# Block products with sums on both sides in the down projections of a two-layer trunk

## The chip, the cores and the metric

The kernel runs on one core of a Trainium2 chip. The metric is the device time of one execution in microseconds, and the median of three runs stands for a kernel. The core has five engines that matter here, each with a queue of its own that it works through in order: TensorE (PE in the profile, its weight loads apart as PEld), VectorE (DVE), ScalarE (ACT), GpSimd (POOL) and SyncE (SP), which issues the loads.

## What is computed

A trunk of two layers over 256 rows (tokens) of 1024 numbers, all in float32. Each layer has a feed-forward block, a token mixer and a second feed-forward block, each between two RMS norms:

```python
def swiglu(h, w_gate_up, w_down):
    gu = h @ w_gate_up                      # 1024 x 5632
    g, u = jnp.split(gu, 2, axis=-1)
    return (jax.nn.silu(g) * u) @ w_down    # 2816 x 1024

for l in range(DEPTH):                      # DEPTH = 2
    h = swiglu(rms_norm(x, ffn1_pre[l]), ffn1_w_gate_up[l], ffn1_w_down[l])
    x = x + 0.5 * rms_norm(h, ffn1_post[l])
    h = hybrid_mixer(rms_norm(x, mix_pre[l]), ...)
    x = x + rms_norm(h, mix_post[l])
    h = swiglu(rms_norm(x, ffn2_pre[l]), ffn2_w_gate_up[l], ffn2_w_down[l])
    x = x + 0.5 * rms_norm(h, ffn2_post[l])
```

The change lies in the four products with `w_down` (the down projections) and in the norm after every block. The mixer (a gated convolution, causal pooling, their projections and an output projection) is as it was, but its output projection goes through the same function.

## The kernel before

**Precision.** Every float32 operand is split into two float32r parts, `hi` (a rounded copy, made by ScalarE) and `lo` (the rest, `raw - hi`, made by VectorE). A product is the sum of three matmuls: hi·hi, hi·lo and lo·hi. Weights are split as they arrive, activations (`split`, `split_pair`) as they are made.

**The weight stream.** All weights of the program form one list of chunks (`stream`, line 89), each 128 partitions x 2048 numbers (1 MB). `issue` (line 108) takes the next chunk of the list: it takes a buffer `hi` and a buffer `lo` (pools `whi` and `wlo`, `LOOK + 1` = 5 buffers each), has SP load the chunk as two halves into two `raw` buffers (pool `raws`, 5 buffers of 128x1024), and puts the splits, a copy on ScalarE and a subtraction on VectorE for each half, into the list `parts`. These are written into the queues of the two engines later, one at a time by `part` between other work, or all of them when `chunk` asks for the next weights. So where a split stands among VectorE's other work is fixed by this code, and a `raw` buffer can take its next load only after its split. `chunk` (line 135) hands out the weights of the next chunk and issues loads until the five buffers are spoken for (`top_up`).

**A feed-forward block** (`ffn`, line 351). Eleven chunks of 256 hidden numbers (`NFU`). For each, two `feat_product` calls (gate and up, 32 matmuls each), sums from PSUM (`add_up`), silu, a multiplication, and `split_pair`, which writes the activations for the down projection into a buffer of the pool `acts`. Then `out_product` (line 275) multiplies: a chunk has two halves of 128 rows of `w_down` (`kk`), two blocks of 128 tokens (`b`) and two halves of 512 output columns (`h`), and each of these eight `step`s is three matmuls of 512 columns, so 24 matmuls a chunk. The results stay in four PSUM banks, `banks[b][h]`, of eight. The first eight chunks go one after the other. The last three (`TAIL`) are held together, so that block 0 is finished first and its norm (`on_block`, which calls `post` and `pre`) runs while TensorE does block 1.

**The norm after a block** (`post`, line 209). ScalarE sums squares of the two banks, VectorE multiplies each bank with a gain into an SBUF tile `u`, POOL makes the reciprocal root `r`, and VectorE computes `x = u * r + x`.

The order on each engine is that of the code (`InOrder`, line 41). The scheduler beneath it only gives out buffers and sets the waits.

Of the kernel before, what the change touches and what calls it, by code (L numbers as in the profile page):

```python
# [10 lines left out]
F32 = mybir.dt.float32  # L11
F32R = mybir.dt.float32r
# [21 lines left out]
WARM = 16  # L34
TURN0 = (9, 11)


F_BG, F_CW, F_PB, F_PS, F_N = 0, 16, 40, 48, 56

# [13 lines left out]
def trunk(ctx: ExitStack, tc: tile.TileContext, x, gains, gcol, feat, wgu1, wd1, win, wco, wpg, wpo, wo, wgu2, wd2, out):  # L53
# [14 lines left out]
    def bank():  # L68
        return psum.tile([P, 512], F32, name="ps")
# [20 lines left out]
    for l in range(DEPTH):  # L90
        for wgu, wd in ((wgu1, wd1), (wgu2, wd2)):
            if wgu is wgu2:
                stream += [("in", l, c) for c in (16, 17, 18, 19)]
                for j in range(4):
                    stream += [("in", l, 4 + j), ("in", l, 8 + j), ("in", l, j)]
                stream += [("in", l, c) for c in (12, 13, 14, 15, 20, 21, 22, 23)]
                stream += [("pg", l, 0)]
                stream += [("co", l, j) for j in range(4)]
                stream += [("po", l, j) for j in range(4)]
                stream += [("o", l, j) for j in range(4)]  # L100
            n = 1 if wgu is wgu1 else 2
            stream += [(f"gu{n}", l, c) for c in range(2 * NFU)]
            stream += [(f"d{n}", l, c) for c in range(NFU)]
    src = {"gu1": wgu1, "d1": wd1, "gu2": wgu2, "d2": wd2, "in": win, "co": wco, "pg": wpg, "po": wpo, "o": wo}
    ready = {}
    state = {"issued": 0, "used": 0}

    def issue(now=True):

        i = state["issued"]  # L110
        state["issued"] = i + 1
        name, l, c = stream[i]
        hi = whi.tile([P, CHUNK], F32R, name="hi")
        lo = wlo.tile([P, CHUNK], F32R, name="lo")
        h = CHUNK // 2
        for s in range(2):
            sl = slice(s * h, (s + 1) * h)
            raw = raws.tile([P, h], F32, name="raw")
            nc.sync.dma_start(raw, src[name][l, c, :, sl])
            parts.append(lambda sl=sl, raw=raw: act.copy(hi[:, sl], raw))  # L120
            parts.append(
                lambda sl=sl, raw=raw: dve.tensor_tensor(lo[:, sl], raw, hi[:, sl].bitcast(F32), op=ALU.subtract)
            )
        ready[i] = (hi, lo)
        if now:
            part(4)

    parts = []

    def part(n=1):  # L130
        for _ in range(n):
            if parts:
                parts.pop(0)()

    def chunk(name, held=0):

        i = state["used"]
        assert stream[i][0] == name, (stream[i], name)
        state["used"] = i + 1
        top_up(held + 1)  # L140
        if state["issued"] == i + 1:
            part(len(parts))
        return ready.pop(i)

    def top_up(held):


        part(len(parts))
        while state["issued"] < min(state["used"] + LOOK + 1 - held, len(stream)):
            part(len(parts))  # L150
            issue(False)

# [115 lines left out]
    def split_pair(src_ap):  # L268
# [6 lines left out]
    def out_product(name, nchunk, acts_hl, on_block):  # L275
        banks = [[bank(), bank()] for _ in range(NB)]
        last = 2 * nchunk - 1

        def step(b, h, kt, w, kk):
            ts_ = slice(b * P, (b + 1) * P)  # L280
            wh, wl = (t.rearrange("p (k c) -> p k c", c=D)[:, kk, HALF[h]] for t in w)
            _, ah, al = acts_hl[kt]
            o = banks[b][h]
            pe.matmul(o, ah[:, ts_], wh, start=(kt == 0), stop=False)
            pe.matmul(o, ah[:, ts_], wl, start=False, stop=False)
            pe.matmul(o, al[:, ts_], wh, start=False, stop=(kt == last))

        for c in range(nchunk - TAIL):
            w = chunk(name)
            for kk in range(2):  # L290
                for b in range(NB):
                    for h in range(2):
                        step(b, h, 2 * c + kk, w, kk)
        ws = []
        for h in range(2):
            for c in range(TAIL):
                if len(ws) <= c:
                    ws.append(chunk(name, c))
                for kk in range(2):
                    step(0, h, 2 * (nchunk - TAIL + c) + kk, ws[c], kk)  # L300
        on_block(0, banks[0])
        n = 0
        for cs in (range(1), range(1, TAIL)):
            for h in range(2):
                for c in cs:
                    for kk in range(2):
                        step(1, h, 2 * (nchunk - TAIL + c) + kk, ws[c], kk)
# [43 lines left out]
    def ffn(l, gu, dn, acts_hl, on_block, gains_):  # L351
# [9 lines left out]
        hs = []  # L361
        for f in range(2, NFU):
            ps = feat_product(gu, acts_hl)
            if f == 2:
                hs += split_pair(turn_back(tok[0]))
            sil = add_up(ps, "sil")
            act.activation(sil, sil, AF.Silu)
            ps = feat_product(gu, acts_hl)
            if f == 2:
                hs += split_pair(turn_back(tok[1]))  # L370
            h = add_up(ps, "h")
            dve.tensor_tensor(h, h, sil, op=ALU.mult)
            hs += split_pair(h)
        gains_()
        out_product(dn, NFU, hs, on_block)

    def mixer(l, acts_hl, on_block, gains_):
        ft = small.tile([P, F_N], F32, name="ft", bufs=1)
# [97 lines left out]
            dve.tensor_tensor(z, z, ga[j], op=ALU.add)  # L476
            merged += split_pair(z)
        gains_()
        out_product("o", 4, merged, on_block)


    plan = []
# [81 lines left out]
    return np.ascontiguousarray(w).reshape(l, k // (2 * P), P, CHUNK)  # L564


def _fill(chunks, at):

    l = chunks.shape[0]
# [45 lines left out]
```

## Time and profile before

| | |
|---|---|
| median of three runs | 1179.0 us (1178.93 to 1180.57) |
| the profiled execution, its own time | 1179.98 us |
| its span, from the first to the last instruction | 1178.2 us |
| TensorE busy | 1165.9 us (99%) |
| VectorE busy | 803.8 us (68%) |
| ScalarE busy | 640.6 us (54%) |
| matmuls | 6192 |
| loaded and stored | 225.00 MB, 191 GB/s over the span |

"Busy" counts an instruction from its start to its end, and in a row of such instructions each begins some 0.08 us before the one ahead of it ends, so that the pace of a row is shorter than the time of one instruction. Line 49 is the wrapper `InOrder`, so instructions are told apart by their tiles: `ps` a PSUM bank, `hi`, `lo` and `raw` weights, `act` activations for an output product, `xt` those for a gate or up product.

### The profile page before, as it was taken

What the parts mean: (1) busy time and instruction counts of PE and PEld (TensorE: products, weight loads), DVE (VectorE), ACT (ScalarE), POOL (GpSimd) and SP (SyncE); (2) the same over time, 40 slices, a digit from 0 to 9 for tenths busy, and PEclk for the clock granted to TensorE, in tenths of its full rate; (3) what the DMA queues carried; (4) which work ended last, traced back from release to release, by engine and by line L of the source; (5) the groups of instructions that cost most, each with busy time, mean ns of one, the idle gap of its engine ahead of it and who ended that gap; (6) DMA issues with size and microseconds to landing.
All of it is one profiled execution on the core that took longest, in us unless ns stands there. A gap on an engine that the chain in (4) does not pass through costs nothing.

```text
span 1178.2 us, 16248 instructions
## 1 busy us (share of the span) xinstructions
PE 1165.9 (99%) x6192; PEld 1002.5 (85%) x6192; DVE 803.8 (68%) x1093; ACT 640.6 (54%) x990; POOL 17.2 (1%) x75
## 2 busy tenths in 40 slices
PE   8999999999999999999999999999999999999997
PEld 5888888888898888888888888888888988888886
DVE  5676745587988777675476766466789886676742
ACT  6655634665565565554365555356556565555630
POOL 0000000000000000000000000000000000000000
PEclk9999999999999999999999999999999999999999
DMA  8666663655566574656456566546565655666540
GB/s 299 216 198 193 194 224 130 245 167 180 170 202 208 169 263 162 193 184 234 159 188 205 182 197 229 189 141 208 178 203 187 200 181 176 200 198 197 190 164 36
DMA packets 62574, 225.00 MB, mean 191 GB/s; under 512 B 7328, under 2 KB 7328, under 8 KB 62496
## 3 DMA queue, kind: packets, MB, share of 16 engines
q1 hardware_dynamic: 62352, 223.96, 57.6%
q8 instruction: 49, 0.80, 0.3%
q14 instruction: 29, 0.24, 0.1%
q10 hardware_dynamic: 144, 0.00, 0.0%
HBM read 222.88 MB, written 1.05 MB: 190 GB/s over the span
## 4 chain that ended last, share of the span: by engine, by line
PE 97%; DVE 1%; ACT 1%; DMA 1%; issue 0%; POOL 0%; SPq 0%; DVEq 0%; POOLq 0%; ACTq 0%
PE ps L49 97%; DVE lo L49 1%; DMA raw<-in_wgu 1%; ACT hi L49 0%; ACT xt L49 0%; ACT junk L49 0%; POOL r L200 0%; DVE x L49 0%; DVE xn L49 0%; DVE v L49 0%; SPq L78 0%; DVEq L611 0%; DVE xt L49 0%; DVE u L49 0%; POOLq L611 0%
## 5 line engine op out<-in xcount | busy, mean ns | idle before, releaser
L49 DVE TENSOR_TENSOR lo<-raw,hi 128x1024 fp32r<-128x1024 f32 x412 | 494.4, 1220 | 134.6 <-ACT hi L49 134.1
L49 ACT CAST hi<-raw 128x1024 fp32r<-128x1024 f32 x412 | 424.5, 1050 | 114.6 <-PE ps L49 89.1
L49 PE MATMUL ps<-xt,hi 128*128 128x512 f32 x1792 | 428.3, 391 | 0.0
L49 PEld LDWEIGHTS ps<-xt,hi 128*128 128x128 f32 x1792 | 329.6, 188 | 64.2
L49 PE MATMUL ps<-hi,act 128*128 128x512 f32 x832 | 259.8, 390 | 0.0
L49 PEld LDWEIGHTS ps<-xt,lo 128*128 128x128 f32 x1792 | 229.8, 191 | 8.7
L49 PE MATMUL ps<-xt,lo 128*128 128x256 f32 x1792 | 232.5, 283 | 0.0
L49 PEld LDWEIGHTS ps<-hi,act 128*128 128x128 f32 x832 | 156.2, 188 | 32.0
L49 PE MATMUL ps<-lo,act 128*128 128x512 f32 x416 | 161.9, 389 | 0.0
L49 ACT COPY h<-ps 128x256 f32<-128x256 f32 x136 | 49.6, 372 | 129.1 <-PE ps L49 128.9
L49 DVE TENSOR_TENSOR h<-ps,h 128x256 f32<-128x256 f32 x136 | 56.2, 422 | 74.7 <-ACT h L49 74.6
L49 PE MATMUL ps<-hi,xt 128*128 128x512 f32 x384 | 100.5, 396 | 3.3 <-ACT hi L49 2.0
L49 PEld LDWEIGHTS ps<-lo,act 128*128 128x128 f32 x416 | 78.2, 188 | 15.7
L49 ACT COPY sil<-ps 128x256 f32<-128x256 f32 x120 | 43.6, 375 | 83.7 <-PE ps L49 83.7
L49 PEld LDWEIGHTS ps<-hi,xt 128*128 128x128 f32 x384 | 71.8, 190 | 18.5 <-ACT hi L49 2.3
L49 PE MATMUL ps<-act,hi 128*128 128x512 f32 (+1 forms) x320 | 72.6, 369 | 0.0
L49 DVE TENSOR_TENSOR sil<-ps,sil 128x256 f32<-128x256 f32 x104 | 42.3, 421 | 42.0 <-ACT sil L49 42.0
L49 ACT CAST act<-h 128x512 fp32r<-128x512 f32 x60 | 37.3, 621 | 60.4 <-DVE h L49 60.4
L49 PEld LDWEIGHTS ps<-act,hi 128*128 128x128 f32 x320 | 57.0, 189 | 9.1
L49 PE MATMUL ps<-lo,xt 128*128 128x512 f32 x192 | 53.9, 399 | 1.2 <-DVE lo L49 1.2
L49 DVE TENSOR_TENSOR act<-h,act 128x512 fp32r<-128x512 f32 (+1 forms) x68 | 46.6, 685 | 6.0 <-ACT act L49 5.7
L49 PEld LDWEIGHTS ps<-lo,xt 128*128 128x128 f32 x192 | 35.8, 189 | 11.3 <-DVE lo L49 4.2
(59 smaller groups left out, 467.4 us busy)
## 6 DMA issues: line engine op xcount, KB each, us to landing
raw<-in_wgu SPq DMA_DIRECT2D x176, 512.0 KB, 4.6
raw<-in_win SPq DMA_DIRECT2D x96, 512.0 KB, 4.7
raw<-in_wd SPq DMA_DIRECT2D x88, 512.0 KB, 4.6
raw<-in_wco SPq DMA_DIRECT2D x16, 512.0 KB, 4.9
raw<-in_wpo SPq DMA_DIRECT2D x16, 512.0 KB, 3.9
raw<-in_wo SPq DMA_DIRECT2D x16, 512.0 KB, 4.7
gain<-in_gains SPq DMA_DIRECT2D x11, 512.0 KB, 4.7
raw<-in_wpg SPq DMA_DIRECT2D x4, 512.0 KB, 3.9
```

Source lines behind the costliest of these rows:

```text
L49: return lambda *a, **kw: self.tc.keep_in_program_order(f(*a, **kw))
```

## The change

Four of the eleven chunks of every down projection (`FAST` = 2, 4, 6, 8) are multiplied in another way. The 256x256 activations and the 256x1024 weights of such a chunk are seen as 2x2 blocks. Seven block products with sums of blocks on both sides replace eight, in the scheme of Strassen and Winograd. So such a chunk has 21 matmuls in place of 24. For this

- VectorE makes four sums of 128x128 of the activations (`forms`), and seven activation blocks are split in place of four;
- VectorE makes four sums of 128x512 of the weights, in place in the two `raw` buffers, after three of the four blocks have been split, and then the buffers are split once more: seven blocks in place of four. Such a chunk takes two buffers of `whi` and `wlo` (`cost` is 2);
- the products go to eight banks in place of four (`extra` holds four of them). The chunks are taken in the order 2, 0, 4, 1, 6, 3, 8, 5, 7, 9, 10. When the last of the four is done, `combine` adds the four extra banks into the four results: one copy on ScalarE and eight additions of 128x512 on VectorE, between the steps of chunk 5;
- the pool `acts` has 16 buffers in place of 12. To make room, `post` leaves the product with the gain in the PSUM bank (no `u`), and the scratch for DMA descriptors is 1 KB;
- the first two column blocks of a fast chunk's weights are swapped on the host.

```diff
+DOWN = (2, 0, 4, 1, 6, 3, 8, 5, 7, 9, 10)
+FAST = (2, 4, 6, 8)
...
-    acts = ctx.enter_context(tc.tile_pool(name="acts", bufs=12))
+    acts = ctx.enter_context(tc.tile_pool(name="acts", bufs=16))
...
+    def cost(i):
+        name, _, c = stream[i]
+        return 2 if name[0] == "d" and c in FAST else 1
...
+        t = new()
+        if cost(i) == 1:
+            for s in range(2):
+                hi(t, s * h, h, s, 0)
+                lo(t, s * h, h, s, 0)
+            ready[i] = t
+        else:
+            t2 = new()
+            q = h // 2
+            b12, b11 = raw[0][:, :q], raw[0][:, q:]
+            b21, b22 = raw[1][:, :q], raw[1][:, q:]
+            for args in ((t, 0, q, 0, q), (t, q, h, 1, 0)):
+                hi(*args)
+            for args in ((t, 0, q, 0, q), (t, q, h, 1, 0)):
+                lo(*args)
+            for o, x, y, op in (
+                (b11, b11, b12, ALU.subtract),
+                (b12, b22, b12, ALU.subtract),
+                (b22, b22, b11, ALU.add),
+                (b21, b21, b22, ALU.subtract),
+            ):
+                parts.append(lambda o=o, x=x, y=y, op=op: dve.tensor_tensor(o, x, y, op=op))
+            for r in range(2):
+                hi(t2, r * h, h, r, 0)
+                lo(t2, r * h, h, r, 0)
+            ready[i] = t + t2
...
-        top_up(held + 1)
+        while state["issued"] <= i:
+            part(len(parts))
+            issue(False)
+        top_up(held + cost(i))
...
-        while state["issued"] < min(state["used"] + LOOK + 1 - held, len(stream)):
+        while state["issued"] < len(stream):
+            ahead = sum(cost(i) for i in range(state["used"], state["issued"] + 1))
+            if held + ahead > LOOK + 1:
+                break
...
-        u = wide.tile([P, D], F32, name="u")
-        mul = lambda s: dve.tensor_tensor(u[:, HALF[s]], banks[s], gain[:, HALF[s]], op=ALU.mult)
+        mul = lambda s: dve.tensor_tensor(banks[s], banks[s], gain[:, HALF[s]], op=ALU.mult)
...
-                xs[b][:, HALF[s]], u[:, HALF[s]], r, xs[b][:, HALF[s]], op0=ALU.mult, op1=ALU.add
+                xs[b][:, HALF[s]], banks[s], r, xs[b][:, HALF[s]], op0=ALU.mult, op1=ALU.add
...
+    def forms(h):
+        a = h.rearrange("p i (b t) -> p (i b) t", b=NB)
...
+        dve.tensor_tensor(sums[:, 0], a[:, 0], a[:, 2], op=ALU.add)
+        dve.tensor_tensor(sums[:, 1], sums[:, 0], a[:, 1], op=ALU.subtract)
+        dve.tensor_tensor(sums[:, 2], a[:, 1], a[:, 0], op=ALU.subtract)
+        dve.tensor_tensor(sums[:, 3], a[:, 3], sums[:, 1], op=ALU.subtract)
...
+        split((fh[:, 0:3], fl[:, 0:3]), a[:, 1:4], 1)
+        split((fh[:, 3:7], fl[:, 3:7]), sums, 1)
+        return fh, fl
...
+        def seven(c, w, last):
+            fh, fl = fast[c]
+            blocks = [t.rearrange("p (q c) -> p q c", c=512) for t in w]
+            for to, a, t, q in ((1, 0, 0, 0), ((1, 0), 2, 0, 1), ((1, 1), 6, 0, 2), (5, 3, 2, 1), (7, 5, 2, 0), (6, 4, 2, 3), ((0, 0), 1, 2, 2)):
...
+                wh, wl = blocks[t][:, q], blocks[t + 1][:, q]
+                matmul(o, to, fh[:, a], wh)
+                matmul(o, to, fh[:, a], wl)
+                matmul(o, to, fl[:, a], wh, last and to in extra)
+
+        def combine():
...
+            act.copy(p1, extra[1])
+            u2 = new("h")
+            dve.tensor_tensor(u2, extra[6], p1, op=ALU.add)
+            yield 1, 0
+            dve.tensor_tensor(banks[1][0], banks[1][0], p1, op=ALU.add)
+            v = new("sil")
+            dve.tensor_tensor(v, u2, extra[5], op=ALU.subtract)
+            yield 1, 1
+            dve.tensor_tensor(banks[1][1], banks[1][1], v, op=ALU.add)
+            u3 = new("h")
+            dve.tensor_tensor(u3, extra[7], u2, op=ALU.add)
+            yield 0, 0
+            dve.tensor_tensor(banks[0][0], banks[0][0], u3, op=ALU.add)
+            v = new("sil")
+            dve.tensor_tensor(v, u3, extra[5], op=ALU.subtract)
+            yield 0, 1
+            dve.tensor_tensor(banks[0][1], banks[0][1], v, op=ALU.add)
...
+            if c in fast:
+                left -= 1
+                seven(c, w, left == 0)
+            elif fast and left == 0:
+                for b, h in combine():
+                    for kk in range(2):
+                        step(b, h, c, w, kk, kk == 1)
+                left = -1
...
-        out_product(dn, NFU, hs, on_block)
+        out_product(dn, DOWN, hs, on_block, fast)
...
-    nc = bacc.Bacc("TRN2", target_bir_lowering=False, num_devices=1)
+    nc = bacc.Bacc("TRN2", target_bir_lowering=False, num_devices=1, dynamic_dma_scratch_size=1024)
```

Where the instructions of the first layer's first down projection stand on VectorE before, from the last hidden chunk's splits to the norm of block 0 (`lo<-raw,hi` is a split of a half chunk of weights, `act<-h,act` the split of the activations, `u<-ps,gain` the norm):

```order
L49 TENSOR_TENSOR h<-ps,h 128x256 x2
L49 TENSOR_TENSOR h<-h,sil 128x512
L49 TENSOR_TENSOR lo<-raw,hi 128x1024
L49 TENSOR_TENSOR act<-h,act 128x2x256
L49 TENSOR_TENSOR lo<-raw,hi 128x1024 x19
L49 TENSOR_TENSOR u<-ps,gain 128x512
```

From the last activations on, nineteen splits of weights follow each other there, and nothing else. The same place in the changed kernel, in two pieces: first from the sums of the last hidden chunk's gate product (`sil<-ps,sil`) to the end of the second fast chunk (`raw<-raw` are the four sums of its weights):

```order
L52 TENSOR_TENSOR lo<-raw,hi 128x512
L52 TENSOR_TENSOR lo<-raw,hi 128x1024
L52 TENSOR_TENSOR raw<-raw 128x512 x4
L52 TENSOR_TENSOR lo<-raw,hi 128x1024 x2
L52 TENSOR_TENSOR sil<-ps,sil 128x256 x2
L52 TENSOR_TENSOR lo<-raw,hi 128x1024 x2
L52 TENSOR_TENSOR h<-ps,h 128x256 x2
L52 TENSOR_TENSOR h<-h,sil 128x512
L52 TENSOR_TENSOR act<-h,act 128x2x256
L52 TENSOR_TENSOR lo<-raw,hi 128x512
L52 TENSOR_TENSOR lo<-raw,hi 128x1024
L52 TENSOR_TENSOR raw<-raw 128x512 x4
```

The first fast chunk's set (three splits' worth, four sums, two splits) now stands ahead of the gate sums of the last hidden chunk, and chunk 0's two splits ahead of its up sums. Then the last fast chunk and the additions of `combine` up to that into the bank of block 0's first half:

```order
L52 TENSOR_TENSOR raw<-raw 128x512 x4
L52 TENSOR_TENSOR lo<-raw,hi 128x1024 x10
L52 TENSOR_TENSOR h<-ps,sil 128x512
L52 TENSOR_TENSOR ps<-ps,sil 128x512
L52 TENSOR_TENSOR sil<-h,ps 128x512
L52 TENSOR_TENSOR ps<-ps,sil 128x512
L52 TENSOR_TENSOR h<-ps,h 128x512
L52 TENSOR_TENSOR ps<-ps,h 128x512
```

Between the last fast chunk's sums and the first addition stand ten splits: two of the fast chunk itself, and two each of chunks 5, 7, 9 and 10, that is all that is left of this down projection.

On TensorE, the end of chunk 5 and the start of the tail, with the buffers' numbers (`ps_1443` is block 0's second half, `ps_1418` its first half, `hi_1599` chunk 7):

```order
L52 MATMUL ps_1443<-lo_1590,act_855 128x512
L52 MATMUL ps_1443<-hi_1589,act_855 128x512 x2
L52 MATMUL ps_1443<-lo_1590,act_855 128x512
L52 MATMUL ps_1443<-hi_1589,act_855 128x512
L52 MATMUL ps_1418<-hi_1599,act_1069 128x512
L52 MATMUL ps_1418<-lo_1600,act_1069 128x512
```

and VectorE's rows that lead to that bank:

```order
L52 TENSOR_TENSOR lo_1665<-raw_1660,hi_1664 128x1024
L52 TENSOR_TENSOR lo_1665<-raw_1662,hi_1664 128x1024
L52 TENSOR_TENSOR h_1678<-ps_1414,sil_1676 128x512
L52 TENSOR_TENSOR ps_1398<-ps_1398,sil_1676 128x512
L52 TENSOR_TENSOR sil_1687<-h_1678,ps_1406 128x512
L52 TENSOR_TENSOR ps_1402<-ps_1402,sil_1687 128x512
L52 TENSOR_TENSOR h_1696<-ps_1410,h_1678 128x512
L52 TENSOR_TENSOR ps_1418<-ps_1418,h_1696 128x512
```

TensorE's first matmul of the tail writes `ps_1418`, the bank that the sixth addition writes. That addition stands behind the splits of chunk 10 (`lo_1665`), which TensorE itself takes up much later. Before, no addition stood between two steps of a bank.

## Rows read from the trace of the kernel before

**Rows 1.** Head of the page: span; busy us, share of the span, instructions.

```profile
span 1178.2 us, 16248 instructions
PE 1165.9 (99%) x6192; PEld 1002.5 (85%) x6192; DVE 803.8 (68%) x1093; ACT 640.6 (54%) x990; POOL 17.2 (1%) x75
...
PE 97%; DVE 1%; ACT 1%; DMA 1%; issue 0%; POOL 0%; SPq 0%; DVEq 0%; POOLq 0%; ACTq 0%
```

**Rows 2.** TensorE's timeline where the first down projection begins: start, us, what.

```profile
136.53 2.08 PE L49 MATMUL ps<-xt,lo 128*128 128x256 f32 x16
138.44 0.40 PE L49 MATMUL ps<-hi,act 128*128 128x512 f32 x1
```

**Rows 3.** Windows: gate/up part; eight down chunks. Length, busy of PE, PEld, DVE, ACT, POOL, PEclk.

```profile
60.00:126.00 66.00, 66.00 (x380) 58.23 (x379) 46.42 (x61) 38.38 (x60) 0.00 (x0) 1.00 0.60 192
138.44:181.96 43.52, 43.52 (x194) 36.05 (x193) 22.82 (x22) 18.84 (x20) 0.00 (x0) 1.00 0.66 219
```

**Rows 4.** VectorE's timeline around the same start: start, us, what, idle before.

```profile
130.12 0.68 DVE L49 TENSOR_TENSOR act<-h,act 128x512 fp32r<-128x512 f32 x1
...
139.05 0.42 DVE L49 TENSOR_TENSOR h<-ps,h 128x256 f32<-128x256 f32 x1 [0.48 <-ACT h L49]
139.51 0.69 DVE L49 TENSOR_TENSOR h<-h,sil 128x512 f32<-128x512 f32 x1
140.12 1.22 DVE L49 TENSOR_TENSOR lo<-raw,hi 128x1024 fp32r<-128x1024 f32 x1
141.25 0.68 DVE L49 TENSOR_TENSOR act<-h,act 128x512 fp32r<-128x512 f32 x1
141.85 5.76 DVE L49 TENSOR_TENSOR lo<-raw,hi 128x1024 fp32r<-128x1024 f32 x5
150.68 2.36 DVE L49 TENSOR_TENSOR lo<-raw,hi 128x1024 fp32r<-128x1024 f32 x2 [3.07 <-ACT hi L49]
```

**Rows 5.** Groups by form: count, busy us, mean ns of one, idle before.

```profile
L49 ACT CAST hi<-raw 128x1024 fp32r<-128x1024 f32 x412 | 424.5, 1050 | 114.6 <-PE ps L49 89.1 <-DMA raw<-in_wgu 18.4 <-DMA raw<-in_win 5.1
L49 ACT CAST act<-h 128x512 fp32r<-128x512 f32 x60 | 37.3, 621 | 60.4 <-DVE h L49 60.4
L49 DVE SCALAR_TENSOR_TENSOR x<-u,r,x 128x512 f32<-128x512 f32 x24 | 17.0, 749 | 1.6 <-POOL r L200 0.5
L49 DVE TENSOR_TENSOR u<-ps,gain 128x512 f32<-128x512 f32 x24 | 16.4, 683 | 20.5 <-ACT junk L49 20.5
L49 DVE SCALAR_TENSOR_TENSOR xt<-ps,gc,xt 128x128 fp32r<-128x128 f32 x16 | 4.4, 343 | 3.3 <-ACT xt L49 3.3
L49 DVE TENSOR_TENSOR h<-h,pool 128x30 f32<-128x30 f32 x2 | 0.4, 191 | 0.1
```

**Rows 6.** The one load of down weights issued at 140 to 142, issue to landing.

```profile
L119 SPq DMA_DIRECT2D raw<-in_wd x1: 328/328/328, 141.4 to 141.4; - x1
...
DMA to landing us min/median/max: 3.6/3.6/3.6
```

**Rows 7.** The five loads issued at 143 to 148, from issue to landing.

```profile
L119 SPq DMA_DIRECT2D raw<-in_wd x5: 328/328/328, 143.1 to 147.6; - x5
...
DMA to landing us min/median/max: 5.0/6.5/6.8
```

**Rows 8.** Waits in the queue of SyncE: us in total, times, longest.

```profile
SPq L119 <- DVE lo L49: 815.1, 341, 13.7
```

**Rows 9.** The program's start, TensorE's timeline: start, us, what, idle before.

```profile
9.27 0.75 PE L49 MATMUL ps<-hi,xt 128*128 128x512 f32 x2 [1.30 <-ACT xt L49]
12.01 0.73 PE L49 MATMUL ps<-hi,xt 128*128 128x512 f32 x2 [1.99 <-ACT hi L49]
```

**Rows 10.** Windows of that start; the seventh column is the granted clock.

```profile
10.00:12.00 2.00, 0.02 (x1) 0.00 (x0) 2.00 (x9) 2.00 (x6) 0.00 (x0) 1.00 1.06 420
12.00:15.00 3.00, 2.99 (x8) 1.97 (x9) 2.11 (x4) 2.97 (x6) 0.00 (x0) 0.61 1.01 391
15.00:18.00 3.00, 2.70 (x10) 1.84 (x8) 2.30 (x6) 2.11 (x3) 0.55 (x1) 0.82 0.87 309
```

More of the change, by code (lines that the diff above doesn't have):

```diff
@@ L102, in trunk @@
             stream += [(f"gu{n}", l, c) for c in range(2 * NFU)]
-            stream += [(f"d{n}", l, c) for c in range(NFU)]
+            stream += [(f"d{n}", l, c) for c in DOWN]
     src = {"gu1": wgu1, "d1": wd1, "gu2": wgu2, "d2": wd2, "in": win, "co": wco, "pg": wpg, "po": wpo, "o": wo}
@@ L112, in issue, with hi, lo @@
         name, l, c = stream[i]
-        hi = whi.tile([P, CHUNK], F32R, name="hi")
-        lo = wlo.tile([P, CHUNK], F32R, name="lo")
         h = CHUNK // 2
+        raw = []
         for s in range(2):
[L117 to L120, printed above, removed]
+            raw.append(raws.tile([P, h], F32, name="raw"))
+            nc.sync.dma_start(raw[s], src[name][l, c, :, s * h : (s + 1) * h])
+        new = lambda: (whi.tile([P, CHUNK], F32R, name="hi"), wlo.tile([P, CHUNK], F32R, name="lo"))
+        def hi(t, at, n, r, off):
+            parts.append(lambda: act.copy(t[0][:, at : at + n], raw[r][:, off : off + n]))
+        def lo(t, at, n, r, off):
             parts.append(
-                lambda sl=sl, raw=raw: dve.tensor_tensor(lo[:, sl], raw, hi[:, sl].bitcast(F32), op=ALU.subtract)
-            )
-        ready[i] = (hi, lo)
+                lambda: dve.tensor_tensor(
+                    t[1][:, at : at + n], raw[r][:, off : off + n], t[0][:, at : at + n].bitcast(F32), op=ALU.subtract
+                )
+            )
+        t = new()
[24 more added lines that the diff above has]
+            ready[i] = t + t2
         if now:
-            part(4)
+            part(len(parts))
     parts = []
@@ L139, in chunk @@
         state["used"] = i + 1
-        top_up(held + 1)
+        while state["issued"] <= i:
+            part(len(parts))
+            issue(False)
+        top_up(held + cost(i))
         if state["issued"] == i + 1:
@@ L272, in split_pair @@
         return [(t[:, i], t[:, i, 0, :], t[:, i, 1, :]) for i in range(2)]
[L275 to L279, printed above, removed]
+    def forms(h):
+        a = h.rearrange("p i (b t) -> p (i b) t", b=NB)
+        sums = tmp.tile([P, 2, T + 2], F32, name="sums", tag="cu", bufs=1)
+        sums = sums.rearrange("p i t -> p (i t)")[:, : 4 * P].rearrange("p (i t) -> p i t", t=P)
+        dve.tensor_tensor(sums[:, 0], a[:, 0], a[:, 2], op=ALU.add)
+        dve.tensor_tensor(sums[:, 1], sums[:, 0], a[:, 1], op=ALU.subtract)
+        dve.tensor_tensor(sums[:, 2], a[:, 1], a[:, 0], op=ALU.subtract)
+        dve.tensor_tensor(sums[:, 3], a[:, 3], sums[:, 1], op=ALU.subtract)
+        fh, fl = (act_slot(F32R).rearrange("p i (x t) -> p (i x) t", t=P) for _ in range(2))
+        split((fh[:, 0:3], fl[:, 0:3]), a[:, 1:4], 1)
+        split((fh[:, 3:7], fl[:, 3:7]), sums, 1)
+        return fh, fl
@@ L280, in step, with out_product, matmul @@
+    def out_product(name, order, acts_hl, on_block, fast={}):
+        nchunk = len(order)
+        banks = [[None, None] for _ in range(NB)]
+        extra = {}
+        began = set()
+        def matmul(o, key, a, w, last=False):
+            pe.matmul(o, a, w, start=key not in began, stop=last, skip_group_check=bool(fast))
+            began.add(key)
+        def step(b, h, c, w, kk, stop=False):
             ts_ = slice(b * P, (b + 1) * P)
             wh, wl = (t.rearrange("p (k c) -> p k c", c=D)[:, kk, HALF[h]] for t in w)
-            _, ah, al = acts_hl[kt]
@@ L283, in step @@
[L283 to L288, printed above, removed]
-            w = chunk(name)
[L290 to L293, printed above, removed]
+            _, ah, al = acts_hl[2 * c + kk]
@@ new lines, in out_product @@
+        left = len(fast)
+        for n, c in enumerate(order[: nchunk - TAIL]):
+            w = chunk(name)
+            if c in fast:
[6 more added lines that the diff above has]
+                left = -1
+            else:
+                for kk in range(2):
+                    for b in range(NB):
+                        for h in range(2):
+                            step(b, h, c, w, kk)
@@ L360, in ffn @@
         fill(gu, acts_hl, take)
-        hs = []
+        hs, fast = [], {}
         for f in range(2, NFU):
@@ L372, in ffn @@
             dve.tensor_tensor(h, h, sil, op=ALU.mult)
-            hs += split_pair(h)
+            if f in FAST:
+                fast[f] = forms(h)
+                hs += [None, None]
+            else:
+                hs += split_pair(h)
         gains_()
-        out_product(dn, NFU, hs, on_block)
+        out_product(dn, DOWN, hs, on_block, fast)
     def mixer(l, acts_hl, on_block, gains_):
@@ L564, in _rows, with _down @@
     return np.ascontiguousarray(w).reshape(l, k // (2 * P), P, CHUNK)
+def _down(w):
+    w = _rows(w)
+    for c in FAST:
+        v = w[:, c].reshape(-1, P, 4, 512)
+        w[:, c] = v[:, :, [1, 0, 2, 3]].reshape(-1, P, CHUNK)
+    return w
 def _fill(chunks, at):
```

23 lines of the change are left out of this document (18 added, 5 removed).

## The prediction

> **What bounds the kernel now.** I read the head of the page first: TensorE is busy 1165.9 us of a span of 1178.2 us and holds 97% of the chain that ended last [rows 1]. So only fewer or shorter matmuls help, and anything that makes TensorE wait is paid in full. Then the timeline of TensorE and VectorE at the first down projection, since the change lies there. TensorE goes from the last gate/up product into the down product without a gap, at 138.44 [rows 2], and stays busy for the whole of the 43.52 us of its first eight chunks [rows 3]. A chunk has 24 matmuls, so one costs 43.52/192 = 0.2267 us (the window's count holds two that straddle its ends). VectorE is busy 22.82 us of these 43.52, ScalarE 18.84 [rows 3]: half of the time they wait for a free buffer, and the weights lie ready. One row shows what this rests on: a pair of splits stands 3.07 us idle, held by the copy to `hi`, which itself waits for TensorE to leave a buffer [rows 4, 5]. Last I looked at the loads, because a `raw` buffer takes its next load only when VectorE has finished with it: SyncE's queue waited 815.1 us for `lo` [rows 8].
>
> **What the change takes away.** Three matmuls for each of four chunks in each of four down projections: 48 x 0.2267 = 10.9 us, all on the path. That would be 1168.1.
>
> **What it adds on VectorE.** Prices by pace: a split of 128x1024 takes (5.76 - 1.22)/4 = 1.135 us in a row of five, a split of 128x512 0.60 (141.25 to 141.85), and an instruction of 128x512 that reads the result of the one before it 0.73 (0.69 and the 0.04 between 139.05 + 0.42 and 139.51) [rows 4]. The in-place sums are not in the trace, but they are float32 additions of 128x512 of the kind that `h<-h,sil` is, and each reads the one before it. So a fast chunk costs 0.60 + 1.14 + 4 x 0.73 + 2 x 1.14 = 6.9 us where a plain one costs 2.27, and TensorE needs 21 x 0.2267 = 4.76 us for it in place of 5.44. A pair of fast and plain takes VectorE 9.2 us, TensorE 10.2. That leaves little, and after the last fast chunk the order puts ten splits and then six additions ahead of TensorE's first matmul of the tail.
>
> I walk VectorE's queue through a down projection, with 0 at TensorE's first matmul of it (138.44 before).
> 1. The split of the second last hidden chunk's activations ends at 130.80 [rows 4], that is -7.6. Behind it now stands chunk 2's set, 6.9: -0.7. The gate sums of the last hidden chunk, 2 x 0.42: 0.1. Chunk 0's splits: 2.4. The two up sums (0.84), the product (0.73), ScalarE's copy of it (0.62 [rows 5] and a hand-over) and its split (0.60): 5.2. Before, this split ended at 3.5 (141.25 + 0.68 [rows 4]).
> 2. The sets of chunks 4, 6 and 8 (20.8) and the splits of 1 and 3 (4.5): 30.5, if nothing waits.
> 3. But a fast chunk holds its two `raw` buffers to its very end, and with five buffers the second half of the next fast chunk can be issued only when the first half of this one is given up. From there VectorE has 1.14 + 2 x 1.14 + 0.60 = 4.0 us of other work, while the load takes 3.6 us alone [rows 6] and its copy 1.05 [rows 5]. I take 0.75 us of waiting ahead of chunks 6 and 8 and 0.3 ahead of chunk 4: the sets end at 32.3, and chunk 8's first `raw` buffer is free at 31.2.
> 4. At 31.2 a burst of five loads begins, 1.14 us apart, as buffers come free: the second half of 7, both of 9, both of 10. The trace has just such a burst, issued from 143.1 to 147.6: the last landed 147.6 + 6.8 = 154.4, 11.3 us after the first was issued [rows 7]. So chunk 10's second half lands at 42.4, its copy and split are done at 44.6. VectorE's own work would have been done at 31.2 + 9 x 1.135 (the second split of 8 and eight more) = 41.4.
> 5. Six additions, half of them reading the one before, 4.0 us: 48.6. Then the first matmul of the tail may start.
>
> TensorE is there at 4 x 4.76 + 4 x 5.44 = 40.8. It waits **7.8 us**, in the first three down projections. In the last one no weights follow, so chunk 10's splits are written behind the additions: these wait for the third load of the burst only (its median wait of 6.5 us from an issue halfway, 145.4, makes it 8.8 after the first [rows 7]): 31.2 + 8.8 + 1.05 + 1.24 + 4.0 = 46.3, a wait of 5.5 us. Together 3 x 7.8 + 5.5 = 28.9 us. Bounds: with the loads landing as soon as VectorE can use them, 45.4 - 40.8 = 4.6, and 2.3 in the last, together 16; each load 1 us later gives 33.
>
> VectorE's order, not its load, makes this: behind the additions nothing is urgent, and ahead of them stand splits that TensorE wants only 2.7 us after the tail has begun.
>
> **The clock.** In the program's start TensorE stood idle for 1.30 us, did two matmuls, stood idle for 1.99 us [rows 9], and then ran at the lower clock (1.2 GHz of 2.4) for part of 12 to 18 us: granted 0.61 over 3 us and 0.82 over 3 us [rows 10], which cost 3 x 0.39 + 3 x 0.18 = 1.7 us of work. A wait of 7.8 us is longer than both, and the tail behind it is on TensorE's path. I take 1.7 us for each of the three long waits, 5.1, and none for the shorter last one; bounds 0 and 3.4 for each. The Trainium skill (TensorE: Matmul & The Clock Gate, "Why this matters for your kernels") says that gaps between bursts of matmuls should be kept short, or the clock goes back; the start of this trace agrees, with 0.61. By that rule the last wait would pay too, 1.7 us more.
>
> **The rest, at nothing.** `forms`: four operations of 128x128 (between 0.19, the 128x30, and 0.34, the 128x128 from PSUM [rows 5]) and a split of seven blocks for four, 1.3 to 1.9 us for each of 16 hidden chunks. VectorE is busy 46.42 of 66 us in that part [rows 3], so it has 3.3 us free of the 11.14 that TensorE takes for a hidden chunk, and ScalarE, with 0.5 us more, 4.7. If that cover went, VectorE would only start the walk later. The norm in PSUM: reading and writing a bank costs what SBUF costs (0.683 for `u`, 0.692 to 0.749 for the others [rows 4, 5]), within 0.1 us each way, and one such chain ends the program; its banks are held 1.4 us longer, while `combine` has freed four. Banks at the start: seven are wanted in the first fast chunk, and the last two still hold the up product until VectorE's sums at about 3.2; the seventh is written at 18 x 0.2267 = 4.1, which leaves 0.9, and a wait there would come off the later one. The scratch size: all loads stand in SyncE's queue, and no row shows one that needs scratch.
>
> **Sum.** 1180.0 (the profiled execution's own time) - 10.9 + 28.9 + 5.1 = 1203.1. The profiled execution lies 1.0 above the median, so **1202**.
>
> **Rivals.**
> - *The clock stays up.* The same waits without 5.1: 1197. For it: at the start the clock was still full while TensorE stood idle from 10 to 12 [rows 10], and how the wait falls is not known. Against: the waits here are four times as long.
> - *The loads don't gate.* If the burst lands as fast as VectorE splits and steps 3 and 4 lose their waits, each wait is 45.4 - 1.8 - 40.8 = 2.8, the last 0.5, too short for the clock: 1179 - 10.9 + 8.9 = 1177. It decides at a fifth landing before 8 us from the first issue. Against: the row says 11.3.
> - *Faster: VectorE is early.* If the walk starts with chunks 2 and 0 already split before 0 (9.2 us earlier), nothing waits, and the 10.9 us come whole: 1168. That needs splits that the code writes behind the last hidden chunks to run ahead of them, and buffers that were free by then; the order speaks against it.
> - *Worse.* Loads 1 us later and the clock at its upper bound in all four: 1179 - 10.9 + 33 + 13.6 = 1215.
>
> **Chances.** The forecast 0.58, the clock staying up 0.22, loads not gating 0.06, early VectorE 0.05, worse 0.09. A measurement can tell about 0.2% (2.4 us) from no change. Slower by more than that: forecast, first and last rival, 0.89; the second rival lies at the edge, 0.04 same and 0.02 faster; with early VectorE, faster is 0.07. The range holds forecast and first rival with the bounds of loads and clock: 1187 (1179 - 10.9 + 16, and some clock) to 1213.
>
> **What would show it.** Right: TensorE idle for 5 to 10 us once in each down projection, at the first matmul into block 0 after chunk 5, released by VectorE's addition into a PSUM bank; a shorter one in the last; ten splits ahead of the first addition, the last ones waiting for a load; matmuls at 0.2267 us elsewhere, and none waiting in the gate/up parts; the granted clock at 0.5 behind the long waits. Wrong: a gap already at the fast chunks (then the sums are dearer than 0.73), gaps in gate/up parts (then `forms` is not covered), or no gap at all.

## The result

The changed kernel takes **1205.3 us** (median of 4 runs, 1203.2 to 1207.8), the kernel before 1179.6 (4 runs beside them): a ratio of 1.0219, with an interval of 1.0207 to 1.0231. It is slower by 25.7 us; 1202 was forecast, with 1187 to 1213 as the range. The profiled execution took 1204.0 us.

The page of the changed kernel, its head, the engines' shares of the chain that ended last, and the group of matmuls that waits (count, busy us, mean ns of one, idle before and what ended it), against [rows 1]:

```profile
span 1202.2 us, 16439 instructions
...
PE 1162.7 (97%) x6144; PEld 997.9 (83%) x6144; DVE 914.4 (76%) x1301; ACT 676.9 (56%) x1042; POOL 17.3 (1%) x75
...
PE 78%; DVE 12%; DMA 5%; ACT 3%; issue 2%; POOL 0%; DVEq 0%; POOLq 0%; SPq 0%; ACTq 0%
...
L52 PE MATMUL ps<-hi,act 128*128 128x512 f32 x800 | 257.2, 399 | 25.6 <-DVE ps L52 25.6
```

The 48 matmuls are gone (6192 before, 6144 now). Yet TensorE holds 78% of the chain where it held 97%, and VectorE and the loads hold 12% and 5%. Nearly all of the lost time comes from one kind of wait, in four places, and from what the clock does behind it. TensorE's timeline at the start of the first down projection and at the first of them (start, us, what, idle before):

```profile
137.97 0.40 PE L52 MATMUL ps<-hi,act 128*128 128x512 f32 x1
...
178.57 0.39 PE L52 MATMUL ps<-hi,act 128*128 128x512 f32 x1
185.41 0.77 PE L52 MATMUL ps<-hi,act 128*128 128x512 f32 x1 [6.46 <-DVE ps L52]
185.98 0.63 PE L52 MATMUL ps<-lo,act 128*128 128x512 f32 x1
```

The row at 185.41 is the first matmul of the tail; what let it go is VectorE's sixth addition. The other three waits are 6.76, 7.66 and 4.77 us. Behind each one the matmuls run at about half their pace: the matmul of the last row lasts 0.63 us, where one lasts 0.39 elsewhere, and the next begins 0.43 us later, not 0.23. The windows show for how long (length, busy of PE, PEld, DVE, ACT, POOL, granted clock, then the DMA's share and its GB/s):

```profile
185.00:188.00 3.00, 2.59 (x6) 2.14 (x7) 2.90 (x5) 1.75 (x2) 0.00 (x0) 0.50 0.24 100
```
```profile
585.20:588.00 2.80, 2.79 (x7) 2.23 (x8) 2.69 (x4) 1.56 (x2) 0.00 (x0) 0.50 0.32 124
588.00:591.20 3.20, 3.20 (x9) 2.53 (x8) 2.99 (x3) 0.00 (x0) 0.00 (x0) 0.50 0.67 223
```
```profile
778.50:782.40 3.90, 3.90 (x9) 3.11 (x10) 3.80 (x5) 1.05 (x1) 0.00 (x0) 0.50 0.15 57
```
```profile
1176.50:1181.70 5.20, 5.16 (x12) 4.13 (x13) 3.44 (x4) 0.00 (x0) 0.00 (x0) 0.50 0.00 0
```

TensorE worked at the lower clock for 3.1, 6.0, 3.9 and 5.2 us after the four waits (in the first place it ends at 188.5), 18.2 us in all, and did half of what it does otherwise: 9.1 us lost. So waits 25.7, clock 9.1, less 10.9 for the matmuls, is 23.9; the spans differ by 24.0. The sum leaves out that the first down projection began 0.5 us earlier than before (137.97 for 138.44 [rows 2]), so the two agree to half a us and not to a tenth.

### The profile page after: what moved, and what is told of

Its sections match the earlier page's. It is cut to its first block, busy times and chain, and to the rows that moved or that the text cites. A ratio compares the mean times of both kernels' runs of the same rounds, so it can differ in the third digit from the quotient of the medians.

```text
span 1202.2 us, 16439 instructions
## 1 busy us (share of the span) xinstructions
PE 1162.7 (97%) x6144; PEld 997.9 (83%) x6144; DVE 914.4 (76%) x1301; ACT 676.9 (56%) x1042; POOL 17.3 (1%) x75
## 4 chain that ended last, share of the span: by engine, by line
PE 78%; DVE 12%; DMA 5%; ACT 3%; issue 2%; POOL 0%; DVEq 0%; POOLq 0%; SPq 0%; ACTq 0%
PE ps L52 78%; DVE lo L52 5%; DMA raw<-in_wd 4%; DVE raw L52 4%; ACT hi L52 2%; DVE h L52 1%; DVE ps L52 1%; DVE sil L52 0%; ACT act L52 0%; DMA x<-in_x 0%; ACT junk L52 0%; ACT xt L52 0%; POOL r L247 0%; DVE xn L52 0%; ACT h L52 0%
## 5 line engine op out<-in xcount | busy, mean ns | idle before, releaser
L52 DVE TENSOR_TENSOR lo<-raw,hi 128x1024 fp32r<-128x1024 f32 (+1 forms) x444 | 523.7, 1201 | 62.1 <-ACT hi L52 61.6
L52 ACT CAST hi<-raw 128x1024 fp32r<-128x1024 f32 (+1 forms) x444 | 450.6, 1034 | 103.7 <-DVE raw L52 49.3
L52 PE MATMUL ps<-hi,act 128*128 128x512 f32 x800 | 257.2, 399 | 25.6 <-DVE ps L52 25.6
L52 PE MATMUL ps<-lo,act 128*128 128x512 f32 x400 | 159.0, 398 | 0.0
L52 DVE TENSOR_TENSOR h<-ps,h 128x256 f32<-128x256 f32 (+1 forms) x140 | 58.6, 429 | 78.4 <-ACT h L52 78.4
L52 ACT COPY sil<-ps 128x256 f32<-128x256 f32 (+1 forms) x124 | 45.5, 382 | 62.9 <-PE ps L52 62.9
L52 ACT CAST act<-h 128x512 fp32r<-128x512 f32 (+1 forms) x60 | 35.6, 593 | 69.4 <-DVE h L52 69.4
L52 DVE TENSOR_TENSOR act<-h,act 128x512 fp32r<-128x512 f32 (+2 forms) x68 | 44.5, 655 | 8.5 <-ACT act L52 8.2
```

The costliest lines, as they stand in the source:

```text
L52: return lambda *a, **kw: self.tc.keep_in_program_order(f(*a, **kw))
```

## The experiments

**The parts that were costed at nothing.** No chunk is fast and the order is the old one; the norm in PSUM, the extra buffer for activations, the new loading code and the scratch size stay.

```diff
-DOWN = (2, 0, 4, 1, 6, 3, 8, 5, 7, 9, 10)
-FAST = (2, 4, 6, 8)
+DOWN = (0, 1, 2, 3, 4, 5, 6, 7, 8, 9, 10)
+FAST = ()
```

> The changed kernel with no fast chunk and the chunks in their old order: what is left of the change is the norm's product in the PSUM bank, 16 activation buffers, the small scratch and the rewritten issue of loads. Mine: these cost nothing, 1179.5 within 1.5. Rival, the norm in PSUM or the scratch costs something in each of six blocks: 1182 or more.

1179.99 us, a ratio of 0.9999 (0.9990 to 1.0009). These parts cost nothing, as forecast.

**The sums on the weights left out.**

```diff
-                parts.append(lambda o=o, x=x, y=y, op=op: dve.tensor_tensor(o, x, y, op=op))
+                pass
```

> The changed kernel without the four in-place sums of the weights of each fast chunk (16 x 4 operations of 128x512 on VectorE left out; the seven products then multiply plain blocks). VectorE's load and order (mine): the sums take 2.8 us for each fast chunk (in the trace 145.07 to 147.85), 11 us in a down projection, more than the wait of 6.5 to 7.7; the additions come before TensorE wants the bank, and the 10.9 us come whole: 1168.6 (1167 to 1171). Rival, the additions between VectorE and TensorE in the banks cost time by themselves: 4 us or more remain in each down projection, 1185 or more. Rival, the loads set the end whatever VectorE does: 1190 to 1200.

1170.28 us, 0.9915 (0.9895 to 0.9934), from two runs. This kernel leaves the sums out, so that its result is no longer the product; it only prices them. No wait for an addition is left, and 10.1 us of the 10.9 come (the kernel before took 1180.4 beside it). Four additions for each fast chunk, 2.8 us each time, decide 35 us. What remains is by which way they do so: VectorE's order, its load, or the loads of weights that they hold back.

**The order: both following chunks behind the additions.** When the additions are written out, the kernel first asks for the next two chunks, and so puts their splits ahead. Here it doesn't.

```diff
-    def chunk(name, held=0):
+    def chunk(name, held=0, more=True):
...
-        top_up(held + cost(i))
+        if more:
+            top_up(held + cost(i))
...
-            w = chunk(name)
+            w = chunk(name, 0, not (fast and left == 0))
```

> The changed kernel, but when chunk 5 is taken up no further splits are written, so that the additions of combine stand ahead of the four splits of chunks 9 and 10 in VectorE's queue (work and loads as they were). Order (mine): in the trace of the changed kernel the split of chunk 7's second half ends at 174.3 and the additions begin at 181.2, so they move 6.9 us forward and the wait of 6.5 us at the start of the tail goes; the splits of 9 and 10 then end at about 180.9, 182.0, 183.2 and 184.3, up to 1.9 us after TensorE wants them, so some 2 us of short waits remain in each down projection and the clock stays up: 1179.5 - 10.9 + 8 = 1177 (1174 to 1182). Rival, VectorE simply has too much work: the same work ends at the same time, 1203 to 1207. Rival, the loads set the end: the tail waits for chunk 10's landing in place of the additions, 5 to 6 us in each, about 1195 to 1200.

1188.42 us, 1.0068 (1.0053 to 1.0083): 16.9 us better than the changed kernel, yet 18.1 above the run without sums, where 1177, some 7 above it, had been expected. The waits of TensorE in that run (us in total, times, longest):

```profile
PE ps L52 <- DVE xn L52: 6.2, 3, 2.3
PE ps L52 <- DVE lo L52: 4.8, 18, 0.6
PE ps L52 <- ACT hi L52: 2.0, 1, 2.0
PE ps L52 <- DVE ps L52: 1.9, 2, 1.6
```

Its timeline, two places behind a down projection:

```profile
181.67 0.51 PE L52 MATMUL ps<-lo,act 128*128 128x512 f32 x1 [0.17 <-DVE lo L52]
182.01 0.64 PE L52 MATMUL ps<-hi,act 128*128 128x512 f32 x2
182.81 0.50 PE L52 MATMUL ps<-lo,act 128*128 128x512 f32 x1 [0.16 <-DVE lo L52]
...
592.54 0.83 PE L52 MATMUL ps<-ident,xn 128*128 128x128 f32 x4 [2.32 <-DVE xn L52]
```

The delay moves on. In the tail TensorE now takes three matmuls for each split of the last chunks, and from 181.67 to 182.81 that is 1.14 us, the pace of VectorE, where three matmuls take 0.68. The row shows 0.17 of idle time; the loss is 0.46. And the norms, which stand behind those splits in VectorE's queue, come later too: the transposes of `xn` wait 1.6 to 2.3 us. So the order is one cause; it is not the only one.

**The loads: a sixth raw buffer.**

```diff
-    raws = ctx.enter_context(tc.tile_pool(name="raws", bufs=5))
+    raws = ctx.enter_context(tc.tile_pool(name="raws", bufs=6))
...
-dynamic_dma_scratch_size=1024
+dynamic_dma_scratch_size=512
```

> The changed kernel with six raw buffers in place of five (the scratch for DMA descriptors is 512 bytes, to make room). Order and loads (mine): one more half chunk is loaded ahead, so the splits of 9 and 10 wait less for their loads; my walk puts 3.2 us of the wait on the burst of loads and 1.8 on the loads ahead of the fast chunks, so the wait falls by 3 to 5 us in each down projection, to some 10 to 14 us in all, with less time at the lower clock: about 1187 (1180 to 1194). Rival, loads don't matter, it is VectorE's own work and order: 1202 to 1207. Rival, the loads are all of it: no wait is left, 1169.

1193.3 us, 1.0110 (1.0095 to 1.0125): 12.0 us better, with the ten splits still ahead of the additions. The waits for the additions are 16.1 us in all in place of 25.6:

```profile
PE ps L52 <- DVE ps L52: 16.1, 4, 5.1
```

So the loads count: with the sixth buffer one load more of this down projection is issued ahead of the burst, which has four of them in place of five, and in the first down projection VectorE no longer waits ahead of the sets of chunks 6 and 8. The scratch of 512 bytes was not run apart.

**Less work for VectorE, same order.** Three fast chunks.

```diff
-DOWN = (2, 0, 4, 1, 6, 3, 8, 5, 7, 9, 10)
-FAST = (2, 4, 6, 8)
+DOWN = (2, 0, 4, 1, 3, 6, 5, 7, 8, 9, 10)
+FAST = (2, 4, 6)
```

(And 15 buffers for activations, not 16.)

> One fast chunk less in each down projection: chunks 2, 4 and 6 are fast, in the order 2, 0, 4, 1, 3, 6, 5, 7, 8, 9, 10; the rest is the changed kernel's. TensorE does 36 products of 0.2267 us less than before in place of 48 (8.2 us in place of 10.9), VectorE has one set of 6.9 us less in each down projection, and between the last set's sums and the first addition there still stand ten splits. Theory (the order and the burst of loads behind the last set make the wait, not the sum of VectorE's work): the wait stays 6 to 7 us in each, and the time is 1208 us (1203 to 1212), 2.7 above the changed kernel for the smaller gain. Rival (VectorE simply has too much work): VectorE comes 6.9 us earlier, TensorE 4.8 (three fast and four plain chunks, 36.0 in place of 40.8), so each wait shrinks by 2.1 us or more, the clock falls for less, and the time is 1198 or less.

1208.6 us, 1.0236 (1.0222 to 1.0250). The waits for the additions are not shorter:

```profile
PE ps L52 <- DVE ps L52: 27.2, 4, 7.2
```

VectorE's timeline there, behind the last sums (start, us, what, idle before):

```profile
162.29 5.84 DVE L52 TENSOR_TENSOR lo<-raw,hi 128x1024 fp32r<-128x1024 f32 x5
168.80 1.23 DVE L52 TENSOR_TENSOR lo<-raw,hi 128x1024 fp32r<-128x1024 f32 x1 [0.68 <-ACT hi L52]
171.11 1.22 DVE L52 TENSOR_TENSOR lo<-raw,hi 128x1024 fp32r<-128x1024 f32 x1 [1.08 <-ACT hi L52]
172.87 1.23 DVE L52 TENSOR_TENSOR lo<-raw,hi 128x1024 fp32r<-128x1024 f32 x1 [0.53 <-ACT hi L52]
174.60 2.41 DVE L52 TENSOR_TENSOR lo<-raw,hi 128x1024 fp32r<-128x1024 f32 x2 [0.51 <-ACT hi L52]
```

Again ten splits, and VectorE stands idle four times among the last five of them, for copies of late loads. VectorE has 6.9 us less to do ahead of them and TensorE is ready 4.8 us earlier. But counted from the first matmul (138.63 here, 137.97 in the changed kernel), VectorE's last sums end only 5.3 us earlier, and the sixth addition only 4.9 (181.00 for 185.27): the waits for copies take the difference, and TensorE waits as long as before. This points to too much ahead of the additions, not too much in all; the next run tests it.

**Three fast chunks, and the order mended.** The two edits above together.

> As the run with three fast chunks, and the order mended: the loads, copies and splits of the two chunks that follow are asked for behind the additions and not ahead of them. Nothing else differs between the two. Theory (the splits ahead of the additions make the wait): no wait is left at the tail, the whole 8.2 us (36 x 0.2267) come, less 1 to 3 us of short waits for late splits: 1173 us (1171 to 1177), faster than both kernels, with the granted clock up at 0.997. Rival (the delay only moves, as the 18 us that were left over the full gain with four fast chunks and this order, since VectorE and the loads are late in any order): half of those 18 remain, 1180 (1178 to 1184).

1177.44 us, 0.9976 (0.9968 to 0.9985). This is 31 us better than the run before it, for the order alone, and faster than both kernels; but it lies between the two forecasts, 2.8 us below the kernel before (1180.3 beside it) and so 5.4 short of the full 8.2. Two of the waits that are left:

```profile
PE ps L52 <- DVE xn L52: 2.5, 3, 1.0
...
PE ps L52 <- DVE ps L52: 1.3, 5, 0.4
```

With 1.9 us for a late `xt`, where the run of the parts alone has 0.8, these make up some 5 us.

**Four fast chunks, six buffers, and the order mended.**

> Four fast chunks, with both mendings: the additions ahead of the splits of the last two chunks, and a sixth buffer for raw weights. The first alone gave 1188.4, the second alone 1193.3, of 1205.3; the full gain with the sums left out is at 1170.3. Theory (two causes: the order holds the additions, and the loads, which find their buffers late, hold the last splits): both together give most of what is missing, 1178 (1174 to 1182). Rival (both only buy VectorE the same few us): 1187 (1185 to 1189), not better than the order alone.

1178.52 us, 0.9985 (0.9976 to 0.9994): 26.8 us better than the changed kernel, of 28.9 (16.9 and 12.0) for the two apart. So the two gains nearly add up, and they are two causes. The waits for `xn` are gone. What is left is the tail. VectorE around the additions, and TensorE in the tail:

```profile
173.56 0.68 DVE L52 TENSOR_TENSOR h<-ps,sil 128x512 f32<-128x512 f32 x1
175.47 0.70 DVE L52 TENSOR_TENSOR ps<-ps,sil 128x512 f32<-128x512 f32 x1 [1.23 <-PE ps L52]
...
178.26 0.70 DVE L52 TENSOR_TENSOR ps<-ps,h 128x512 f32<-128x512 f32 x1
```
```profile
181.52 0.50 PE L52 MATMUL ps<-lo,act 128*128 128x512 f32 x1 [0.42 <-DVE lo L52]
```

VectorE is now early at the additions and stands idle 1.23 us for TensorE, while TensorE later waits for splits. One pair of splits could stand ahead.

**One chunk ahead of the additions, one behind.** As the run before, with this in place of its order:

```diff
-            w = chunk(name)
+            w = chunk(name, 1 if fast and left == 0 else 0)
```

> Four fast chunks and six raw buffers, and only the second of the two chunks that follow is put behind the additions; the first (chunk 9) is asked for ahead of them. In the run with both behind, VectorE began the additions at 173.56 us and then stood idle 1.23 us for chunk 5's matmuls, and the sixth addition ended at 178.96, when TensorE reached the tail at 179.5; then TensorE took three matmuls (0.68 us) for each split (1.13 us) of chunks 9 and 10, which cost 1.6 us in each down projection. Theory (the place of the splits is a trade of few us: each pair ahead holds the additions 2.27 us longer, each pair behind holds the tail): two splits ahead use up the 1.23 us and 0.5 us of slack and leave a wait of 0.5 to 1 us at the additions, while the 1.6 us go: 1176 us (1174 to 1178), faster than both kernels. Rival (chunk 9's splits wait for their loads, and the additions behind them too, as with all ten splits ahead, where VectorE stood idle for 0.86 and 1.12 us for copies of late loads): a wait of 2 us or more in each, 1181 (1179 to 1185).

**1174.97 us, 0.9958 (0.9944 to 0.9971)**, the fastest here: 5.1 us below the kernel before and 30 below the changed one. With six buffers, ten splits ahead of the additions gave 1193.3 us, six gave 1178.5, and eight give this. TensorE's waits for additions are 4.7 us in all four places; the second row is the one in the first place:

```profile
PE ps L52 <- DVE ps L52: 4.7, 4, 1.5
```
```profile
180.33 0.47 PE L52 MATMUL ps<-hi,act 128*128 128x512 f32 x1 [1.34 <-DVE ps L52]
```

**The clock.** TensorE is kept at work through its wait: one product into the bank to which VectorE adds last is repeated 25 times (18 in the last down projection), and the result moves by that.

```diff
             matmul(o, key, ah[:, ts_], wl)
+            for _ in range(again):
+                matmul(o, key, al[:, ts_], wh)
             matmul(o, key, al[:, ts_], wh, stop or (c, kk) == (order[-1], 1))
...
+        state["downs"] = state.get("downs", 0) + bool(fast)
+        again = 18 if state["downs"] == 4 else 25
...
-                        step(b, h, c, w, kk, kk == 1)
+                        step(b, h, c, w, kk, kk == 1, again if (b, h, kk) == (0, 1, 1) else 0)
```

> The changed kernel, with TensorE kept at work through its wait: the last product of chunk 5 for the bank that VectorE adds to last is added 25 times more (18 in the last down projection). It is the product of the low parts of the activations with the high parts of the weights, and the output moves by that. 25 x 0.2267 = 5.7 us of the waits of 6.5, 6.8 and 7.7 us are so filled, 4.1 of the 4.8 us in the last, and the additions come when they came. It prices the clock: whatever the lower clock costs behind the waits comes off, and nothing else changes. Theory (the lower clock cost 9.1 us in the four places: 1.5, 3.0, 1.9 and 2.6, by the time that the matmuls behind each wait ran at half the clock): 1196 us (1194 to 1198), granted clock 0.997 or more. The forecast's price of 5.1 us: 1200. Rival (the matmuls at the lower clock would have waited for late splits anyway): 1205.

1200.15 us (1197.7 to 1203.2), 1.0169 (1.0152 to 1.0187): 5.2 us come back although TensorE does 93 matmuls more. The repeated matmuls by themselves only add time, and in the rows below the additions come no earlier. So the lower clock costs time, and the rival of 1205 falls. That 1200 is also what the forecast's price gives is no support for that price: waits and repeated matmuls together grew too. The profiled execution shows how much. It is the slowest of the four, 1203.2 us, at a granted clock of 0.994; the others took 1197.7 to 1201.9 at 0.996 and 0.997. Its waits for additions are

```profile
PE ps L52 <- DVE ps L52: 8.4, 4, 3.6
```

and with 93 x 0.2267 = 21.1 us of repeated matmuls that is 29.5, 3.8 more than the changed kernel's 25.7. The clock fell again behind two of the rests that remained (2.22 us at 187.49, 3.60 at 589.96), and not behind the third (2.42 at 782.46):

```profile
187.50:191.00 3.50, 3.50 (x9) 2.78 (x10) 3.40 (x5) 0.56 (x1) 0.00 (x0) 0.52 0.08 27
```
```profile
590.00:594.00 4.00, 4.00 (x11) 3.14 (x12) 3.90 (x5) 0.84 (x1) 0.00 (x0) 0.57 0.19 57
...
782.50:786.00 3.50, 3.50 (x16) 2.90 (x17) 3.40 (x5) 1.92 (x2) 0.00 (x0) 1.00 0.29 98
```

At 0.52 and 0.57 these two cost 3.5 x 0.48 = 1.7 and 4.0 x 0.43 = 1.7 us, 3.4 in place of 9.1. The first down projection began 0.7 us later (138.62 for 137.97). So 5.7 less, 3.8 and 0.7 more: 1.2 us less than the changed kernel's profiled execution, and 0.8 was measured. In the first place the sixth addition ended 2.1 us later (187.35 for 185.27): 0.7 is that later start, 0.9 are longer waits ahead of the sets, the rest lies at the burst. Why these loads came later stays open.

## Why the prediction was right, point by point

The time was right to 3 us and the mechanism in its place. But two terms were off, the waits by 3.2 us too much and the clock by 4.0 too little, and that they cancelled is luck. Here is VectorE's queue at the first down projection of the changed kernel, where TensorE's first matmul stands at 137.97, the walk's 0:

```profile
129.28 0.69 DVE L52 TENSOR_TENSOR act<-h,act 128x512 fp32r<-128x512 f32 x1 [0.69 <-ACT act L52]
...
134.41 2.43 DVE L52 TENSOR_TENSOR lo<-raw,hi 128x1024 fp32r<-128x1024 f32 x2
...
142.45 0.69 DVE L52 TENSOR_TENSOR act<-h,act 128x512 fp32r<-128x512 f32 x1 [0.69 <-ACT act L52]
...
143.92 1.23 DVE L52 TENSOR_TENSOR lo<-raw,hi 128x1024 fp32r<-128x1024 f32 x1 [0.18 <-ACT hi L52]
...
153.48 1.22 DVE L52 TENSOR_TENSOR lo<-raw,hi 128x1024 fp32r<-128x1024 f32 x1 [0.33 <-ACT hi L52]
...
162.99 1.23 DVE L52 TENSOR_TENSOR lo<-raw,hi 128x1024 fp32r<-128x1024 f32 x1 [0.29 <-ACT hi L52]
...
166.91 5.83 DVE L52 TENSOR_TENSOR lo<-raw,hi 128x1024 fp32r<-128x1024 f32 x5
173.04 1.22 DVE L52 TENSOR_TENSOR lo<-raw,hi 128x1024 fp32r<-128x1024 f32 x1 [0.30 <-ACT hi L52]
175.52 1.23 DVE L52 TENSOR_TENSOR lo<-raw,hi 128x1024 fp32r<-128x1024 f32 x1 [1.25 <-ACT hi L52]
177.31 1.23 DVE L52 TENSOR_TENSOR lo<-raw,hi 128x1024 fp32r<-128x1024 f32 x1 [0.56 <-ACT hi L52]
178.79 2.48 DVE L52 TENSOR_TENSOR lo<-raw,hi 128x1024 fp32r<-128x1024 f32 x2 [0.26 <-ACT hi L52]
...
184.57 0.70 DVE L52 TENSOR_TENSOR ps<-ps,h 128x512 f32<-128x512 f32 x1
```

- *Step 1*: the second last split ends at -8.0 (forecast -7.6), chunk 2's set at -1.1 (-0.7), the last hidden chunk's split at 5.2 (5.2). Right.
- *Steps 2 and 3*: the row at 166.91 begins with the two splits of chunk 8's sums, so its first raw buffer is free at 168.1, or 30.2; forecast 31.2. **The waits ahead of the sets were the mis-sized term**: 0.8 us (0.18 + 0.33 + 0.29), not 1.8, in part because the loads waited for there landed in 3.3 us (149.09 to 152.37, 158.65 to 161.89), not 3.6.
- *Step 4*: SyncE's queue then issues the burst. The first is issued at 168.2; the rows of the other four, and their time to landing:

```profile
L125 SPq DMA_DIRECT2D raw<-in_wd x4: 327/328/328, 169.4 to 172.8; - x4
...
DMA to landing us min/median/max: 5.0/5.8/6.2
```

  The last landed at 172.8 + 6.2 = 179.0, 10.8 us after the first was issued; forecast 11.3, from [rows 7]. The ten splits end at 181.27, or 43.3; forecast 44.6.
- *Step 5*: the sixth addition ends at 185.27, 4.0 us later, as forecast. TensorE was ready at 178.80, or 40.8, as forecast. So the wait is 6.5 us and not 7.8: 1.0 of the 1.3 is step 3's, the rest the burst's.
- *The four waits*: 25.7 us, not 28.9. The last one is 4.8, forecast 5.5: shorter than the others, as the code's order said.
- *"VectorE's order, not its load, makes this"*: half right. Less work in the same order gained nothing (1208.6). But the order alone is worth 16.9 us, the buffer 12.0, both 26.8: the late loads, which steps 3 and 4 had, are a cause beside the order. *"Behind the additions nothing is urgent"* was wrong: splits put there hold the tail's matmuls and the next block's transposes.
- *The clock*: 9.1 us, not 5.1. This step failed by its size, at both points: 1.7 for each wait came from a start in which the clock fell once and early, and the last wait was costed at nothing because it is shorter, though 4.8 us idle cost 2.6. The Trainium skill (TensorE: Matmul & The Clock Gate, "Why this matters for your kernels") says that gaps between bursts of matmuls should be kept short, or the clock goes back. By that rule the last wait pays too, and the trace agrees, with 0.50 over 5.2 us. The rival in which the clock stays up is out.
- *The prices*: right. The sums last 0.69 us each, and four take 2.86 from start to end (4 x 0.73 = 2.92 forecast); the norm's product in PSUM takes 0.692 (0.683 for `u` in [rows 5]). Two groups by form of the changed kernel:

```profile
L52 DVE TENSOR_TENSOR raw<-raw 128x512 f32<-128x512 f32 x64 | 44.2, 690 | 1.6
...
L52 DVE TENSOR_TENSOR ps<-ps,gain 128x512 f32<-128x512 f32 x24 | 16.6, 692 | 12.3 <-ACT junk L52 12.3
```

With the two terms as measured the sum is 1180.0 - 10.9 + 25.7 + 9.1 = 1203.9, and the profiled execution took 1204.0. The rival of 1168, in which VectorE is early, is what the run with sums left out comes near to (1170.3); the best order gets about half of the way from the kernel before (1175.0).

## What to carry to other kernels

Work that one engine does in place of another's is not paid by its busy time (VectorE was at 68%, and 76% fits too) but by the place in its queue from which the waiting engine is let go: walk that queue to the instruction that releases it, and count what stands ahead. A buffer held to the end of a longer set of operations delays the loads that need it and the work behind them, here for 12.0 us; order and buffers have to be mended together. And put work behind the release only as far as it isn't wanted soon: eight splits ahead were better than ten and than six. Where the waiting engine's clock falls behind a wait, add it for every wait, the shorter one of 4.8 us too: here 9.1 us to 25.7 of waiting.

## What the runs showed that had not been expected

- Rests of nearly the same length at TensorE were followed by the lower clock or not: after 2.22 us at 187.49 and 3.60 us at 589.96 it was 0.52 and 0.57, after 2.42 us at 782.46 it stayed at 1.00, in one execution. In the first run with the additions ahead of both chunks 2.20 us at 781.59 were followed by 1.00, and 2.32 us at 592.54 by 0.62 over 4.5 us:

```profile
592.50:597.00 4.50, 4.46 (x17) 3.69 (x18) 2.57 (x3) 1.88 (x3) 0.00 (x0) 0.62 0.00 0
```

- At the lower clock TensorE stayed for 3.1 to 6.0 us after it had started again, longest not behind the longest wait (6.0 behind 6.76 us, 3.9 behind 7.66).
- The program's start, in which the clock fell before [rows 10], ran at full clock in the profiled execution of the changed kernel, which reached its first down projection 0.5 us earlier:

```profile
12.00:15.00 3.00, 2.84 (x12) 1.87 (x12) 2.01 (x3) 2.97 (x6) 0.00 (x0) 1.00 1.00 399
```
